# Gate and up products of a decoder layer: features by the row, or tokens by the row with seven block products in place of eight

## The chip, the cores and the metric

The kernel runs on one core of a Trainium2 chip. Its engines are TensorE (PE in the rows; PEld is its load of the stationary operand), VectorE (DVE), ScalarE (ACT), GpSimd (POOL) and the queue that issues the loads (SP). The metric is the device time of one execution in microseconds (us). Before the change the median of three runs is 1202.92 us, from 1201.81 to 1204.26.

## The reference

One decoder layer over 256 tokens of width 2048, in float32. A mixer (a gated linear recurrence beside differential attention) is followed by a norm; then come a SwiGLU network with 5632 hidden features, a second norm, a gate on a per-layer input, and a third norm. The change is in the SwiGLU:

```python
def swiglu(h, w_gate, w_up, w_down):
    g = jnp.einsum('bsd,df->bsf', h, w_gate)
    u = jnp.einsum('bsd,df->bsf', h, w_up)
    return jnp.einsum('bsf,fd->bsd', jax.nn.silu(g) * u, w_down)
...
        h = layer_norm(ALPHA * h + m, ln1_g[i], ln1_b[i])
        f = swiglu(h, w_ffn_gate[i], w_ffn_up[i], w_ffn_down[i])
        h = layer_norm(ALPHA * h + f, ln2_g[i], ln2_b[i])
```

## The kernel before, in words

**Numbers in two parts.** TensorE multiplies rounded operands, so each operand is split into a high and a low part, and a product is three: high by high, high by low, low by high. For a weight the high part `wh` is a copy on ScalarE (L114) and the low part `wl` a subtraction on VectorE (L106), both 1024 columns wide.

**Weight units.** The weights come in units of 128 rows by 2048 columns, 1 MB each, one load per unit on SP (L96) into three buffers. `Stream` splits a unit in halves of 1024 columns. Six pairs of `wh` and `wl` exist, so the high part of a half can be written when TensorE is done with the half six places earlier (`room`, L116).

**Ticks.** The order of the program is the order in which Python emits it; nothing is rescheduled. TensorE's work is cut into quarters of a unit. After each quarter `tick` (L127) emits one stage of every job that is under way (a job is a generator, and a `yield` ends a stage), then the low part of the next half and the high part of the one after it. Each engine works through its own list in order, and waits for others by semaphores.

**Gate and up before.** The 44 tiles of 128 features run in three parts of 16, 16 and 12 (`FPARTS`). `feature_major` (L199) makes the tile's product with features on the rows of the result: for each of 16 row tiles, one instruction with 512 columns (the weight's high part by both parts of `x1`, L196) and one with 256 (the low part by the high part of `x1`, L197). The job `swiglu` (L759) adds the two halves of a bank, applies silu to gate, multiplies by up, and writes both parts of the product into `hT`, which the down projection takes as its stationary operand. The down projection is `token_major` (L226): tokens on the rows, 24 instructions of 512 columns a unit, in two banks.

**Banks.** The pool `pm` has four PSUM banks, taken in turn; `aux` has two, and `sc` is one tile of two banks. The per-layer inputs (`ple_unit`, L731) stand in the `pm` banks and in `sc` just ahead of the SwiGLU, and the script of the first norm (`norm_to`, L651, with `NORM1`) copies them to `ev` in its steps `v` (L695), the last of them in the second tick of the SwiGLU.

## Time and profile before

| | |
|---|---|
| median of three runs | 1202.92 us |
| span of the profiled execution, first to last instruction | 1199.7 us |
| rest of the median around that span | 3.2 us |
| PE busy | 1182.0 us (99%) |
| PEld busy | 1008.2 us (84%) |
| DVE busy | 775.7 us (65%) |
| ACT busy | 607.5 us (51%) |
| POOL busy | 34.3 us (3%) |
| mean DMA rate | 196 GB/s |

The profile lists each instruction with its start and its duration. Instructions of one engine overlap at their ends, so the step from one start to the next is shorter than the duration, and it is the step that adds up. A wait is shown in brackets as the engine's idle time and what ended it. The granted TensorE clock is shown as a share of 2.4 GHz.

### The profile page before, as it was taken

What the parts mean: (1) busy time and instruction counts of PE and PEld (TensorE: products, weight loads), DVE (VectorE), ACT (ScalarE), POOL (GpSimd) and SP (SyncE); (2) the same over time, 40 slices, a digit from 0 to 9 for tenths busy, and PEclk for the clock granted to TensorE, in tenths of its full rate; (3) what the DMA queues carried; (4) which work ended last, traced back from release to release, by engine and by line L of the source; (5) the groups of instructions that cost most, each with busy time, mean ns of one, the idle gap of its engine ahead of it and who ended that gap; (6) DMA issues with size and microseconds to landing.
All of it is one profiled execution on the core that took longest, in us unless ns stands there. A gap on an engine that the chain in (4) does not pass through costs nothing.

```text
span 1199.7 us, 15640 instructions
## 1 busy us (share of the span) xinstructions
PE 1182.0 (99%) x6210; PEld 1008.2 (84%) x6210; DVE 775.7 (65%) x1066; ACT 607.5 (51%) x945; POOL 34.3 (3%) x60
## 2 busy tenths in 40 slices
PE   9999999999999999999999999999999999999995
PEld 7888888888888888888888888888888888887885
DVE  6976988785678555564455555554455555556977
ACT  6767576664456454443335444443344454435640
POOL 0000000001010000000000000000000000002001
PEclk9999999999999999999999999999999999999998
DMA  9765454547638555555555555555555555554741
GB/s 332 263 219 196 174 176 148 181 164 287 235 119 315 183 203 177 200 186 197 189 199 187 176 189 196 176 181 205 186 200 176 190 196 175 182 204 150 281 166 70
DMA packets 38872, 234.83 MB, mean 196 GB/s; under 512 B 4432, under 2 KB 8440, under 8 KB 12048
## 3 DMA queue, kind: packets, MB, share of 16 engines
q1 hardware_dynamic: 35952, 221.51, 52.7%
q0 software_dynamic: 2848, 12.34, 2.7%
q8 instruction: 48, 0.79, 0.2%
q14 instruction: 24, 0.20, 0.0%
HBM read 231.72 MB, written 3.68 MB: 196 GB/s over the span
## 4 chain that ended last, share of the span: by engine, by line
PE 94%; DVE 3%; ACT 1%; POOL 1%; DMA 1%; issue 0%; SPq 0%; DVEq 0%; POOLq 0%; ACTq 0%
PE u L196 13%; PE g L196 13%; PE u L197 7%; PE g L197 7%; PE dps L223 7%; PE dps L224 7%; PE dps L222 6%; PE ops L222 2%; PE ops L223 2%; PE ops L224 2%; PE xr L196 2%; PE k L196 2%; PE yg L196 2%; PE q L196 2%; PE gps L223 2%; PE gps L222 2%
## 5 line engine op out<-in xcount | busy, mean ns | idle before, releaser
L106 DVE TENSOR_TENSOR wl<-w,wh 128x1024 fp32r<-128x1024 f32 x404 | 493.0, 1223 | 277.3 <-ACT wh L114 271.3
L114 ACT CAST wh<-w 128x1024 fp32r<-128x1024 f32 x404 | 423.9, 1052 | 309.3 <-PE dps L224 143.7
L196 PE MATMUL u<-x,wh 128*128 128x512 f32 x688 | 243.4, 396 | 0.0
L196 PE MATMUL g<-x,wh 128*128 128x512 f32 x688 | 243.4, 396 | 0.0
L197 PE MATMUL u<-x,wl 128*128 128x256 f32 x688 | 193.0, 281 | 0.0
L197 PE MATMUL g<-x,wl 128*128 128x256 f32 x688 | 193.0, 281 | 0.0
L196 PEld LDWEIGHTS u<-x,wh 128*128 128x128 f32 x688 | 129.1, 188 | 30.8
L196 PEld LDWEIGHTS g<-x,wh 128*128 128x128 f32 x688 | 129.1, 188 | 30.8
L222 PE MATMUL dps<-wh,hT 128*128 128x512 f32 x352 | 137.1, 389 | 0.0
L224 PE MATMUL dps<-wh,hT 128*128 128x512 f32 x352 | 137.0, 389 | 0.0
L223 PE MATMUL dps<-wl,hT 128*128 128x512 f32 x352 | 137.0, 389 | 0.0
L197 PEld LDWEIGHTS g<-x,wl 128*128 128x128 f32 x688 | 130.0, 189 | 0.1
L197 PEld LDWEIGHTS u<-x,wl 128*128 128x128 f32 x688 | 130.0, 189 | 0.0
L222 PEld LDWEIGHTS dps<-wh,hT 128*128 128x128 f32 x352 | 66.1, 188 | 13.8
L223 PEld LDWEIGHTS dps<-wl,hT 128*128 128x128 f32 x352 | 66.1, 188 | 13.6
L224 PEld LDWEIGHTS dps<-wh,hT 128*128 128x128 f32 x352 | 66.1, 188 | 13.6
L212 ACT COPY g<-g 128x256 f32<-128x256 f32 x43 | 16.0, 372 | 79.4 <-PE g L197 79.4
L212 ACT COPY uu<-u 128x256 f32<-128x256 f32 x43 | 16.0, 373 | 77.0 <-PE u L197 77.0
L222 PE MATMUL ops<-wh,mhl 128*128 128x512 f32 x128 | 50.3, 393 | 0.0
L223 PE MATMUL ops<-wl,mhl 128*128 128x512 f32 x128 | 49.9, 390 | 0.0
L224 PE MATMUL ops<-wh,mhl 128*128 128x512 f32 x128 | 49.9, 390 | 0.0
L196 PE MATMUL xr<-xhl,wh 128*128 128x512 f32 x128 | 46.5, 406 | 1.6 <-ACT wh L71 1.5
(227 smaller groups left out, 1598.6 us busy)
## 6 DMA issues: line engine op xcount, KB each, us to landing
w<-in_w_gate SPq DMA_DIRECT2D x44, 1024.0 KB, 4.9
w<-in_w_up SPq DMA_DIRECT2D x44, 1024.0 KB, 4.8
w<-in_w_down SPq DMA_DIRECT2D x44, 1024.0 KB, 4.9
w<-in_w_a SPq DMA_DIRECT2D x28, 1024.0 KB, 4.9
w<-in_w_out SPq DMA_DIRECT2D x16, 1024.0 KB, 4.9
w<-in_w_pg SPq DMA_DIRECT2D x16, 1024.0 KB, 5.0
w<-in_w_v SPq DMA_DIRECT2D x8, 1024.0 KB, 4.9
lng<-in_ln_g POOLq DMA_DIRECT2D x3, 1024.0 KB, 5.9
```

What stands on the lines that cost most here:

```text
L106: self.nc.vector.tensor_tensor(wl, self.source(self.los), wh.bitcast(F32), ALU.subtract)
L114: self.nc.scalar.copy(wh, src)
L196: nc.tensor.matmul(ps, wh[:, c], xhl[:, k, :], start=(k == 0), stop=False)
L197: nc.tensor.matmul(ps[:, :S], wl[:, c], xhl[:, k, :S], start=False, stop=(k == KT - 1))
L212: nc.scalar.copy(out, ps[:, S:])
L222: nc.tensor.matmul(ps, ah, wh[:, c], start=first, stop=False)
L223: nc.tensor.matmul(ps, ah, wl[:, c], start=False, stop=False)
L224: nc.tensor.matmul(ps, al, wh[:, c], start=False, stop=last)
```

## The change

**Tokens on the rows.** `gate_up` takes four feature tiles at a time (a group, 11 in all). A unit now holds two row tiles of gate and of up for 512 features; it is loaded by two DMAs of 512 KB whose contiguous runs are 1 KB, where there was one with runs of 8 KB. For each row tile, token half and weight, `product` issues three instructions of 512 columns, with `x1` stationary. Four banks `q[token half][gate or up]` hold the sums.

**Seven products.** In the last two of a group's eight units the two row tiles and the two token halves, by gate and up, form a product of 2 by 2 blocks, done with seven block products in place of eight (Strassen's scheme in Winograd's form). Its operands are sums: of `x1`, made once after the first norm (`sums_of_x1`), and of the weights, made on VectorE (`add_up`). Such a unit is split into four parts: gate, one quarter of up, and two of sums. Three of the products go straight into `q`, the others into `p1`, `p6`, `p5`, `p7`.

**The end of a group.** The job `finish` starts in the group's last unit. It adds the banks up, applies silu, multiplies, turns the product by eight transpositions on TensorE (two of four), and splits it into `hT`.

**Room.** `ev` goes to DRAM and comes back after the SwiGLU, since its tiles (tag `T`) hold the sums of weights in between; the sums of `x1` take the place of the norm's `g` and `b` (tag `gb`), and the second norm's are loaded in the third part. Small buffers share one tag of seven (`tmp`).

```diff
+SEVEN = 2
...
-            self.order[2 * n:2 * n + 4] = [(n, 0), (n + 1, 0), (n, 1), (n + 1, 1)]
+        self.sevens = sevens
+        self.order = [(n, j) for n in range(len(srcs)) for j in range(4 if n in sevens else 2)]
...
+            if isinstance(self.srcs[n], tuple):
+                for i, src in enumerate(self.srcs[n]):
+                    dst = w[:, i * 1024:(i + 1) * 1024].rearrange("p (f c) -> p f c", f=4)
+                    self.nc.sync.dma_start(dst, src)
...
+        if n in self.sevens and j:
+            if j == 1:
+                return self.blocks(n)[:, 1, :, 1, :], 512
+            return self.sums[n][:, (j - 2) * 1024:(j - 1) * 1024], 1024
+        return self.w32[n][:, j * 1024:j * 1024 + 1024], 1024
...
+    def add_up(self, n, j):
+        add = lambda out, a, b: self.nc.vector.tensor_tensor(out, a, b, ALU.add)
+        b = self.blocks(n)
+        if j == 0:
+            self.sums[n] = self.sums_pool.tile([P, 2048], F32, tag="T", name="sums", bufs=2)
+        t = self.sums[n].rearrange("p (i f c) -> p i f c", i=4, f=4)
+        if j == 0:
+            w = self.w32[n]
+            diagonal = bass.AP(w.tensor, w.offset, [w.ap[0], [1024 + P, 2], [2 * P, 4], [1, P]])
+            add(t[:, 0:2], diagonal, b[:, 1, :, 0, :].unsqueeze(1).broadcast_to([P, 2, 4, P]))
+        else:
+            t1, t2, t4 = t[:, 0], t[:, 2], t[:, 3]
+            add(t2, t1, b[:, 1, :, 1, :])
+            add(t4, t2, b[:, 0, :, 1, :])
...
+        self.released += j == 1
...
+        self.nc.scalar.copy(self.shaped(wh, src, cols), src)
+        if n in self.sevens and j < 2:
+            self.add_up(n, j)
...
-        srcs += [t[n][f0 + i] for i in range(nf) for n in ("w_gate", "w_up")]
+        for f in range(f0, f0 + nf, 4):
+            sevens.update(range(len(srcs) + PAIRS - SEVEN, len(srcs) + PAIRS))
+            srcs += [tuple(t[w][f:f + 4, :, 2 * P * j:2 * P * (j + 1)].rearrange("f p c -> p f c")
+                           for w in ("w_gate", "w_up")) for j in range(PAIRS)]
...
-                us[h, b] = late.tile([P, 512], F32, tag="u", name="u", bufs=2)
+                us[h, b] = tmp("u")
...
+                elif a == "E":
+                    for h in range(2):
+                        nc.gpsimd.dma_start(evd[h], ev[h])
...
+    def sums_of_x1():
+        xsum.append(late.tile([P, SEVEN, 4, 2, P], F32R, tag="gb", name="xsum"))
+        work = act.tile([P, 2 * SEVEN * 512], F32, tag="A", name="work")
+        x, sums = work[:, :SEVEN * 512], work[:, SEVEN * 512:]
+        ks = slice(KT - 2 * SEVEN, KT)
+        nc.vector.tensor_tensor(x.rearrange("p (k s) -> p k s", s=S), x1[:, ks, :S].bitcast(F32),
+                                x1[:, ks, S:].bitcast(F32), ALU.add)
+        yield
+        a11, a21, a12, a22 = (x.rearrange("p (m i c) -> p m i c", i=4, c=P)[:, :, i, :] for i in range(4))
+        s1, s3, s2, s4 = (sums.rearrange("p (m i c) -> p m i c", i=4, c=P)[:, :, i, :] for i in range(4))
+        nc.vector.tensor_tensor(s1, a22, a21, ALU.subtract)
+        nc.vector.tensor_tensor(s3, a11, a21, ALU.subtract)
+        yield
+        nc.vector.scalar_tensor_tensor(s2, s1, -1.0, a11, ALU.mult, ALU.subtract)
+        nc.vector.tensor_tensor(s4, a12, s2, ALU.add)
+        yield
+        sums = sums.rearrange("p (n c) -> p n c", c=P)
+        hi, lo = (xsum[0].rearrange("p m i a c -> p (m i) a c")[:, :, a, :] for a in range(2))
+        nc.scalar.copy(hi, sums)
+        yield
+        nc.vector.tensor_tensor(lo, sums, hi.bitcast(F32), ALU.subtract)
...
+    def product(ps, a, w, first, last):
+        out = ps.rearrange("p (f c) -> p f c", c=P)
+        nc.tensor.matmul(out, a[0], w[0], start=first, stop=False)
+        nc.tensor.matmul(out, a[0], w[1], start=False, stop=False)
+        nc.tensor.matmul(out, a[1], w[0], start=False, stop=last)
...
+    def gate_up(hT, i0):
+        n0 = st.take(PAIRS)
+        q = [[bank("gu") for _ in range(2)] for _ in range(2)]
+        for m in range(PAIRS - SEVEN):
+            for g in range(2):
+                for h in range(2):
+                    for i in range(2):
+                        k = 2 * m + i
+                        a = [x1[:, k, o + h * P:o + (h + 1) * P] for o in (0, S)]
+                        product(q[h][g], a, operand(n0 + m, g, i), m + i == 0,
+                                g * h * i == 1 and m == PAIRS - SEVEN - 1)
+                    st.free(h)
+                    st.tick()
+        pp = [aux("p1"), aux("p6")]
+        both = pa.tile([P, 2, 512], F32, tag="sc", name="p57")
+        p1, p6, p5, p7 = pp[0], pp[1], both[:, 0, :], both[:, 1, :]
+        for m in range(PAIRS - SEVEN, PAIRS):
+            n, first, last = n0 + m, m == PAIRS - SEVEN, m == PAIRS - 1
+            def x(h, i):
+                return [x1[:, 2 * m + i, o + h * P:o + (h + 1) * P] for o in (0, S)]
+            def sx(i):
+                return [xsum[0][:, m - PAIRS + SEVEN, i, a, :] for a in range(2)]
+            product(q[0][0], x(0, 1), operand(n, 0, 1), False, last)
+            product(p1, x(0, 0), operand(n, 0, 0), first, last)
+            if last:
+                if hT is None:
+                    hT = act.tile([P, KT, 2 * S], F32R, tag="A", name="hT")
+                st.start(finish(hT, i0, q, p1, p6, p5, p7))
+            st.free()
+            st.tick()
+            product(q[0][1], sx(3), operand(n, 1, 0), False, last)
+            st.free()
+            product(p5, sx(0), operand(n, 2, 0), first, last)
+            st.tick()
+            product(p7, sx(1), operand(n, 2, 1), first, last)
+            st.free()
+            product(q[1][0], x(1, 1), operand(n, 3, 1), False, last)
+            st.tick()
+            product(p6, sx(2), operand(n, 3, 0), first, last)
+            st.free()
+            st.tick()
+        return hT
+    def finish(hT, i0, q, p1, p6, p5, p7):
+        add = lambda out, a, b, op=ALU.add: nc.vector.tensor_tensor(out, a, b, op)
+        yield
+        g0 = tmp("g0")
+        nc.scalar.copy(g0, q[0][0])
+        yield
+        u0 = tmp("u0")
+        nc.scalar.copy(u0, q[0][1])
+        add(g0, p1, g0)
+        u1 = tmp("u1")
+        nc.scalar.copy(u1, q[1][1])
+        yield
+        g1, u2, u3 = tmp("g1"), tmp("u2"), tmp("u3")
+        nc.scalar.copy(g1, q[1][0])
+        nc.scalar.copy(u2, p6)
+        nc.scalar.activation(g0, g0, AF.Silu)
+        yield
+        add(u2, p1, u2)
+        add(u3, p7, u2)
+        add(u2, p5, u2)
+        yield
+        add(g1, g1, u3)
+        add(u3, p5, u3)
+        add(u0, u0, u2, ALU.subtract)
+        nc.scalar.activation(g1, g1, AF.Silu)
+        yield
+        add(u1, u1, u3, ALU.subtract)
+        add(g0, g0, u0, ALU.mult)
+        yield
+        add(g1, g1, u1, ALU.mult)
+        for h, g in enumerate((g0, g1)):
+            tp = aux("tp")
+            for i in range(4):
+                nc.tensor.transpose(tp[:, i * P:(i + 1) * P], g[:, i * P:(i + 1) * P], ident)
             yield
+            tp = tp.rearrange("p (a b) -> p a b", b=P)
+            hi, lo = (hT[:, i0:i0 + 4, o + h * P:o + (h + 1) * P] for o in (0, S))
+            nc.scalar.copy(hi, tp)
+            yield
+            nc.vector.tensor_tensor(lo, tp, hi.bitcast(F32), ALU.subtract)
...
-                gps, ups = feature_major(x1, "g"), []
-                st.start(swiglu(gps, ups, hT, i))
-                ups.append(feature_major(x1, "u"))
...
+        for i0 in range(0, nf, 4):
+            hT = gate_up(hT, i0)
         nq = nf // 4
         end = part == len(FPARTS) - 1
+        if end:
+            gb = load_gb(2)
...
+    ev = [late.tile([P, D], F32, tag="T", name="ev", bufs=2) for _ in range(2)]
...
+    ev = [late.tile([P, D], F32, tag="T", name="ev", bufs=2) for _ in range(2)]
+    for h in range(2):
+        nc.gpsimd.dma_start(ev[h], evd[h])
```

On TensorE, where one group ends and the next begins (in words: the last product of a group is `p6`, here `p_3714`; behind it come 24 instructions of the next group and then the first transposition). Before, the list holds the two forms of `feature_major` at this place:

```order
L197 MATMUL u<-x_3149,wl 128x256
L196 MATMUL u<-x_3149,wh 128x512
L197 MATMUL u<-x_3149,wl 128x256
L196 MATMUL g<-x_3149,wh 128x512
L197 MATMUL g<-x_3149,wl 128x256
L196 MATMUL g<-x_3149,wh 128x512
```

After, around the first transposition of the first group's product:

```order
L847 MATMUL gu<-wl,x_3150 128x512
L848 MATMUL gu<-wh,x_3150 128x512
L846 MATMUL gu<-wh,x_3150 128x512
L847 MATMUL gu<-wl,x_3150 128x512
L848 MATMUL gu<-wh,x_3150 128x512
L939 MATMUL tp<-ident,g_3774 128x128 x4
L846 MATMUL gu<-wh,x_3150 128x512
L847 MATMUL gu<-wl,x_3150 128x512
L848 MATMUL gu<-wh,x_3150 128x512
```

The pairs of 512 and 256 columns are gone, all are 512, and TensorE has a row of four transpositions that reads `g0` of the group just ended, 24 instructions into the next.

On VectorE, at the end of a feature tile before (`g` and `uu` are gate and up, `hT` the low part of the product):

```order
L214 TENSOR_TENSOR g<-g 128x256
L106 TENSOR_TENSOR wl<-w_3695,wh 128x1024
L106 TENSOR_TENSOR wl<-w_3744,wh 128x1024
L214 TENSOR_TENSOR uu<-u,uu 128x256
L768 TENSOR_TENSOR g<-g,uu 128x256
L106 TENSOR_TENSOR wl<-w_3744,wh 128x1024
L772 TENSOR_TENSOR hT<-g,hT 128x256
L106 TENSOR_TENSOR wl<-w_3791,wh 128x1024
```

After, from the end of the first group's last product to `g0`'s product with up (`p_3713` is `p1`, `p_3715` is the tile of `p5` and `p7`, `u_3802` and `u_3803` are `u2` and `u3`, `g_3774` is `g0`, `g_3801` is `g1`, `u_3789` and `u_3792` are `u0` and `u1`):

```order
L147 TENSOR_TENSOR wl<-w_3660,wh 128x1024 x2
L907 TENSOR_TENSOR u_3802<-p_3713,u_3802 128x512
L907 TENSOR_TENSOR u_3803<-p_3715,u_3802 128x512
L907 TENSOR_TENSOR u_3802<-p_3715,u_3802 128x512
L147 TENSOR_TENSOR wl<-w_3734,wh 128x1024
L907 TENSOR_TENSOR g_3801<-g_3801,u_3803 128x512
L907 TENSOR_TENSOR u_3803<-p_3715,u_3803 128x512
L907 TENSOR_TENSOR u_3789<-u_3789,u_3802 128x512
L147 TENSOR_TENSOR wl<-w_3734,wh 128x1024
L907 TENSOR_TENSOR u_3792<-u_3792,u_3803 128x512
L907 TENSOR_TENSOR g_3774<-g_3774,u_3789 128x512
L907 TENSOR_TENSOR g_3801<-g_3801,u_3792 128x512
```

Where two or three additions stood between two low parts, seven additions of 512 columns, two products and the low parts of weights now stand in one run, and the row that the first transposition reads (`g_3774`, L907, next to last) is the tenth row, counted from the first that reads `p1` and `u2`.

On ScalarE, at the same place, after (`gu` is a bank of `q`, `p_3714` is `p6`; before, a copy of a bank, a silu or a high part of `hT`, all of 256 columns, stood between two high parts of weights):

```order
L156 CAST wh<-w_3660 128x1024
L913 COPY u_3789<-gu 128x512
L916 COPY u_3792<-gu 128x512
L156 CAST wh<-w_3660 128x1024
L919 COPY g_3801<-gu 128x512
L920 COPY u_3802<-p_3714 128x512
L921 ACT_TABLE_LOAD
L921 ACTIVATE g_3774<-g_3774 128x512
L156 CAST wh<-w_3734 128x1024 x2
L930 ACTIVATE g_3801<-g_3801 128x512
```

The copies out of five banks and two silu now stand between the high parts of the next group's weights.

## Rows read from the trace of the kernel before

**Rows 1.** Page, the chain that ended last, share of the span by engine.
```profile
PE 94%; DVE 3%; ACT 1%; POOL 1%; DMA 1%; issue 0%; SPq 0%; DVEq 0%; POOLq 0%; ACTq 0%
```

**Rows 2.** Windows: stage, length, busy of PE, PEld, DVE, ACT, POOL; clock, DMA, GB/s.
```profile
359.40:536.99 177.59, 177.59 (x1028) 156.59 (x1026) 110.69 (x136) 91.84 (x135) 1.14 (x2) 1.00 0.59 210
536.99:624.07 87.08, 87.08 (x387) 72.07 (x385) 44.18 (x42) 34.41 (x34) 0.00 (x0) 1.00 0.56 194
624.07:804.96 180.89, 180.89 (x1026) 156.96 (x1024) 103.98 (x127) 86.79 (x126) 0.00 (x0) 1.00 0.54 186
804.96:892.06 87.10, 87.10 (x386) 72.10 (x385) 44.17 (x42) 34.42 (x34) 0.00 (x0) 1.00 0.57 195
892.06:1027.73 135.67, 135.67 (x769) 117.72 (x768) 77.94 (x95) 64.92 (x94) 0.00 (x0) 1.00 0.54 186
```

**Rows 3.** Timeline of PE, 354 to 360 us: start, duration, instruction.
```profile
354.86 0.39 PE L224 MATMUL eps<-wh,phl 128*128 128x512 f32 x1
355.15 0.66 PE L681 MATMUL tp<-ident,z 128*128 128x128 f32 x4
355.56 0.48 PE L222 MATMUL eps<-wh,phl 128*128 128x512 f32 x1
355.88 0.40 PE L223 MATMUL eps<-wl,phl 128*128 128x512 f32 x1
...
359.40 0.48 PE L196 MATMUL gu<-x,wh 128*128 128x512 f32 x1
```

**Rows 4.** Timeline of ACT, 359 to 363 us.
```profile
359.83 0.61 ACT L695 COPY ev<-eps 128x512 f32<-128x512 f32 x1
360.31 0.62 ACT L684 CAST x<-tp 128x512 fp32r<-128x512 f32 x1
360.79 1.09 ACT L114 CAST wh<-w 128x1024 fp32r<-128x1024 f32 x1
361.73 1.12 ACT L695 COPY ev<-eps 128x512 f32<-128x512 f32 x2
```

**Rows 5.** Timeline of PE and ACT, 558 to 559 us, down projection.
```profile
558.56 0.39 PE L224 MATMUL dps<-wh,hT 128*128 128x512 f32 x1
...
558.99 1.05 ACT L114 CAST wh<-w 128x1024 fp32r<-128x1024 f32 x1 [1.67 <-PE dps L224]
```

**Rows 6.** Timeline of DVE, 1109 to 1113 us.
```profile
1109.28 0.69 DVE L693 TENSOR_TENSOR x<-y,x 128x512 fp32r<-128x512 f32 x1
1109.89 0.69 DVE L697 TENSOR_TENSOR z<-z,lng 128x512 f32<-128x512 f32 x1
1110.61 0.69 DVE L698 TENSOR_TENSOR z<-z,lnb 128x512 f32<-128x512 f32 x1
1111.21 1.22 DVE L106 TENSOR_TENSOR wl<-w,wh 128x1024 fp32r<-128x1024 f32 x1
1112.35 0.68 DVE L693 TENSOR_TENSOR x<-y,x 128x512 fp32r<-128x512 f32 x1
```

**Rows 7.** Lines by form: busy, mean ns of one, idle before and its releaser.
```profile
L642 DVE TENSOR_TENSOR z<-z,dps 128x512 f32<-128x512 f32 x16 | 10.5, 679 | 3.1 <-PE dps L224 3.1
L764 ACT ACTIVATE g<-g 128x256 f32<-128x256 f32 x44 | 18.5, 420 | 0.4 <-DVE g L214 0.4
L106 DVE TENSOR_TENSOR wl<-w,wh 128x1024 fp32r<-128x1024 f32 x404 | 493.0, 1223 | 277.3 <-ACT wh L114 271.3 <-PE u L196 3.1
```

**Rows 8.** Page's DMA issues and DMA of 9 to 17 us: KB each, us to landing.
```profile
w<-in_w_gate SPq DMA_DIRECT2D x44, 1024.0 KB, 4.9
...
DMA packets 2420, 2.94 MB, mean 367 GB/s; under 512 B 146, under 2 KB 1826, under 8 KB 2420
...
w<-in_w_a SPq DMA_DIRECT2D x3, 384.0 KB, 7.2
```

**Rows 9.** Windows, with the columns of rows 2: a wait in the second norm.
```profile
1090.00:1094.00 4.00, 2.62 (x14) 1.74 (x13) 2.83 (x4) 1.21 (x3) 3.33 (x4) 1.00 0.00 0
```

More of the change, by code (lines that the diff above doesn't have):

```diff
@@ L108, in prepare_lo @@
+    def prepare_lo(self):
+        n, j = self.order[self.los]
+        wh, wl = self.parts[n, j]
+        src, cols = self.source(self.los)
+        wh, wl = (self.shaped(t, src, cols) for t in (wh, wl))
+        self.nc.vector.tensor_tensor(wl, src, wh.bitcast(F32), ALU.subtract)
+        self.released += j == 1
         self.los += 1
@@ L649, in residuals, with norm_to @@
             yield
-    def norm_to(script, xhl, pss, scale, stats, gb, cols):
+    def norm_to(script, xhl, pss, scale, stats, gb, cols, then=None):
         mvs, us, tps = {}, {}, {}
@@ L694, in step @@
             elif what == "v":
-                nc.scalar.copy(ev[:, h, c], inputs[b][h])
+                nc.scalar.copy(ev[h][:, c], inputs[b][h])
             elif what == "r":
@@ L711, in norm_to @@
         st.held = False
+        if then is not None:
+            yield from then()
     gb = load_gb(1)
@@ L774, in tile_hybrid_layer @@
-    for part, (f0, nf) in enumerate(FPARTS):
-        hT = act.tile([P, KT, 2 * S], F32R, tag="A", name="hT")
-        for i in range(nf):
-            if part == 0 and i == 0:
-                gps, ups = feature_major(x1, "gu", 2)
-                st.start(swiglu(gps, [ups], hT, i))
-                gb = load_gb(2)
-            else:
-                gps, ups = feature_major(x1, "g"), []
-                st.start(swiglu(gps, ups, hT, i))
-                ups.append(feature_major(x1, "u"))
+    def product(ps, a, w, first, last):
[3 more added lines that the diff above has]
+        nc.tensor.matmul(out, a[1], w[0], start=False, stop=last)
@@ new lines, in operand @@
+    def operand(n, j, i):
+        parts = st.half(n, j)
+        if n in st.sevens and j:
+            return [w[:, i * 512:(i + 1) * 512].rearrange("p (f c) -> p f c", c=P) for w in parts]
+        return [w.rearrange("p (f k c) -> p f k c", f=4, k=2)[:, :, i, :] for w in parts]
+    def gate_up(hT, i0):
[40 more added lines that the diff above has]
+        return hT
@@ L810, in gated @@
         n = cols.stop - cols.start
[L811 removed]
+        g = tmp("pg")[:, :n]
         nc.vector.tensor_tensor(g, ps[:, :n], pb[:, cols], ALU.add)
```

73 lines of the change are left out of this document (33 added, 40 removed).

## Prediction

> **What bounds the kernel now.** I read the chain of waits first: 94% of the span lies on TensorE and 1% on loads [rows 1]. The windows by stage come next: in all three gate/up stages and in the down stages between them TensorE is busy for the whole stage at the full clock, VectorE for 57 to 62% in gate and up (110.69 of 177.59 us, 103.98 of 180.89, 77.94 of 135.67) and ScalarE for about half [rows 2]. So before the change time goes by TensorE's instructions alone, and a change pays there if it takes instructions off TensorE and adds no wait in front of one. The later rows price both.
>
> **The matmuls.** A down stage is 16 units of 24 instructions of 512 columns, 384 in 87.08 us [rows 2]: 0.2268 us each. The three gate/up stages last 177.59 + 180.89 + 135.67 = 494.15 us for 88 units [rows 2]. After the change these units are instructions of the same 512 columns with x1 stationary, 24 a unit, so I price them like those of the down stage. 66 units of 24 and 22 units of 21 make 2046, and 2046 x 0.2268 = 464.0 us. The gain is 30.1 us. Half of it comes from the form (2112 x 0.2268 = 479.0, 15.2 us less than 494.15), half from the 66 instructions that Strassen's scheme drops (15.0 us). The weights are now read in runs of 128 columns and the result is written as four such runs; no row shows that form, and I take the price of the plain one.
>
> **The transpositions.** Each group adds eight, in two rows of four. Around such a row of four in the first norm, the matmul before starts at 354.86 and the second one behind at 355.88 [rows 3]: 1.02 us where two steps would be 0.45, so 0.57 us a row. 22 rows at 0.55 make 12.1 us.
>
> **The wait in front of the first transposition.** This is the term that decides. The transposition of g0 is emitted four ticks into the next group, 24 x 0.2268 = 5.44 us after TensorE leaves the group's last product p6. By then VectorE must have run the ten rows of its list from the addition of p1 and u2 to the product of g0 and u0, which the list after the change shows, two low parts of weights among them. I count from TensorE's end of p6.
> ScalarE starts 0.43 us after the start of the matmul that it waits for (558.99 against 558.56) [rows 5], so 0.20 us after the step ends. Its copy of p6 to u2 starts at 0.20 at the earliest and takes 0.60: done at 0.8 [rows 4]. What stands before it on ScalarE doesn't hold it much longer: from the release of a half at -4.56 (21 instructions earlier, and 0.20 for the release) it runs a high part, a copy, a high part and two copies; with steps of 0.94 for a high part and 0.48 for a copy (360.79 to 361.73, 360.31 to 360.79) [rows 4] the last high part starts at -1.24, the copy of q10 at -0.30, that of p6 at 0.2. VectorE's low part for that last high part runs from -0.16, and the next row may start 1.14 later [rows 6], at 1.0.
> VectorE's steps: 0.61 from one 512-column row to an independent one, 0.72 to one that needs its result, 1.14 for a low part [rows 6]. The addition to u2 takes 0.72 (the next needs it), the two others 0.61 each, a low part 1.14, three additions 1.83, a low part 1.14, an addition 0.61, and the last row, the product, its full 0.69: 7.35 us. An addition that reads PSUM lasts 0.68 as well [rows 7], so I make no difference between them. VectorE is done at 1.0 + 7.35 = 8.35, TensorE arrives at 5.44: it waits 2.9 us. It happens at each of the 11 groups, also where the down projection follows, since a tick is six instructions there too: 31.9 us.
> From below: with every row independent, starting at 0.8, the sum is 0.8 + 7 x 0.61 + 2 x 1.14 + 0.69 = 8.0, a wait of 2.6. From above: each addition with a handover (0.74), each low part at its full 1.22, and ScalarE late by one high part (0.94) give 1.9 + 5.2 + 2.4 + 0.7 = 10.2, a wait of 4.8. I take 2.9, by the steps as the rows show them, and keep 28 and 53 us as ends. Behind the first transposition stand the second (12 instructions later, its product is one row further on VectorE, ready at about 9) and the next units, whose halves are ready by then; they add nothing. The silu of g1 (0.42 us for 256 columns [rows 7], an estimate of 0.8 at most for 512) ends before the product that needs it.
>
> **The start.** The four banks of the first group are those in which the per-layer inputs stood, and the third, q[1][0], is needed after six instructions, not after two units. TensorE began at 359.40 [rows 3], so it wants the bank at 360.9; the last two copies to ev run from 361.73 for 1.12 us [rows 4]. A wait of 2.0 us, once.
>
> **What I cost at nothing.** Per group VectorE has 12 low parts of plain units, and for each of the two special ones three of 1024 and one of 512 columns, one sum of 1024 and two of 512; with ten rows and two low parts at the end that is 20 rows at 1.14 and 18 at 0.61, 34 us of some 46. So it keeps up over a group, and the backlog of the wait is gone before the next special units; uncovered, a late half costs its 1.14 us on TensorE. The sums of x1 have some 30 us before their first use. The way of ev to DRAM and back on POOL's queue stands behind the second norm's first scale and ahead of its second, with room of several microseconds; the ends of both norms are otherwise the same. The loads keep their bytes, 1 MB per unit, but half of the three buffers' lead goes in the special units: the load of the third unit of the next group is issued some 7 us before its first high part, and a load lands in 4.9 us [rows 8].
> The loads are now two of 512 KB in runs of 1 KB. At the start, where loads of 384 KB in runs of up to 1 KB fill the queue, the DMA engines moved 367 GB/s [rows 8], and gate and up need 186 to 210 [rows 2], so I add nothing. The Trainium skill (DMA: Bandwidth & Descriptors, section "Bandwidth") advises DMAs of 1 MiB and more and shows far lower rates for small ones, 138 GB/s at 64 KB; at that rate, an estimate by the page, a unit would take 7.6 us to land where TensorE needs 5.44, and loads would become the bound. The trace speaks against it, since the queue overlaps neighbouring loads.
>
> **The sum.** -30.1 + 12.1 + 31.9 + 2.0 = +15.9 us on the profiled span of 1199.7 us. The median of the runs is 3.2 us over that span, so 1202.9 + 15.9 = 1218.8 us. With the ends of the wait (28 and 53), 11 to 13 for the transpositions and 1 to 3 for the start, the likeliest case runs from +10 to +39: 1213 to 1242.
>
> **The rivals.**
> A, faster. TensorE doesn't wait at the transposition. The point from which it decides is 16.0 / 11 = 1.45 us a group: VectorE must finish the product within 6.9 us of p6. VectorE's idle time in gate and up (some 40%) [rows 2] speaks for it, of which nearly all is a wait for ScalarE's high parts (271.3 of 277.3 us before the low parts) [rows 7], so low parts may be done earlier than I count; against it stands that the ten rows can't start before p6 is copied, whatever went before. Without any wait: -30.1 + 12.1 + 2.0 = -16.0, 1187 us.
> B, no change. The wait is half as long, as if the two low parts were out of the way: 8.35 - 2.28 = 6.1, a wait of 0.6, or of 1.5 with ScalarE late by one high part. With 11 such waits 1194 to 1204 us, about 1202.
> C, slower still. The special units starve too: eight halves (9.1 us of low parts) fall due in their 9.5 us, with ScalarE's five copies between, and a load that comes late holds ScalarE's list and all behind it. One high and low part per group, 2.2 us, makes +24: 1243 us.
> D, the clock. Each wait lets TensorE fall to the 1.2 GHz level. In the second norm it stood idle for 1.4 of 4 us and the granted clock stayed 1.00 [rows 9]; if instead six instructions a group ran at half the clock, that adds 1.36 x 11 = 15 us: 1234. The Trainium skill (TensorE: Matmul & The Clock Gate, section "HAM oscillation") has a kernel whose regular idle gaps brought the clock down each time; no wait as long as 2.9 us with work on both sides is in this trace.
>
> **How the numbers follow.** Forecast 67%, A 14%, B 7%, C 9%, D 3%. The time is 1218.8 us. B, the nearer part of A, D and the forecast's own range up to 1240 are taken into the range, 1200 to 1240, which leaves out some 12% below and 7% above. What this kernel's measurement can tell from no change is about 0.2%, 2.4 us. Faster: A and three of B's seven, 17%. Same: the rest of B and 2% of the forecast's lower edge, 6%. Slower: 77%.
>
> **What would show it.** Matmuls of gate and up at steps of 0.227 us, 2046 of them; transpositions with TensorE idle 2.5 to 3.5 us before the first of each group, released by VectorE's product (L907), and none before the second; no wait on a DMA; PEclk at 1.00 throughout; 2 us of idle time at the second bank block of the first group, released by the copy to ev. It would be wrong if the first transposition found g0 ready, if the matmuls with weights in runs of 128 columns took longer than 0.227, or if TensorE waited on halves of weights in the special units.

## The result and the profile after

The changed kernel takes 1235.76 us (median of four runs, 1234.59 to 1236.05), the kernel before 1202.44 us on the same chip (four runs): a ratio of 1.0265, 95% interval 1.025 to 1.0279. It is slower by 33.3 us, where the forecast was 1218.8 us, slower by 15.9. The time lies in the range, the sign is right, and the loss is a little over twice the forecast's. The span grew from 1199.7 to 1233.8 us, by 34.1.

The page of the kernel after: busy time of TensorE, its granted clock in 40 slices, and the chain of waits, the counterpart of [rows 1].
```profile
PE 1179.6 (96%) x5528; PEld 981.0 (80%) x5528; DVE 879.1 (71%) x1138; ACT 633.0 (51%) x913; POOL 36.0 (3%) x64
...
PEclk9999999999999999999999999999999999999998
...
PE 83%; DVE 10%; ACT 4%; issue 2%; POOL 1%; DMA 0%; SPq 0%; DVEq 0%; ACTq 0%; POOLq 0%
```
TensorE's part of the chain fell from 94 to 83%, and VectorE now holds 10%. The clock by slices looks untouched, since a slice is 31 us long: a fall of a few microseconds does not show there. The waits of TensorE say where VectorE comes in (total us, times, longest):
```profile
PE tp L939 <- DVE g L907: 36.2, 11, 4.1
```
There is one wait for each of the 11 groups, in front of the first transposition, and it ends with VectorE's product (L907), as the prediction named it. TensorE waits for nothing else in the SwiGLU, neither a half of a weight nor a load. The loads of 512 KB land fast (page: KB each, us to landing):
```profile
w<-in_w_gate SPq DMA_DIRECT2D x88, 512.0 KB, 3.6
w<-in_w_up SPq DMA_DIRECT2D x88, 512.0 KB, 4.7
```
The windows by stage, with the columns of [rows 2]: gate and up of the first part, and its down projection.
```profile
359.15:545.97 186.82, 176.32 (x772) 145.19 (x771) 143.19 (x157) 99.12 (x120) 1.15 (x2) 0.97 0.59 193
545.97:638.65 92.68, 89.46 (x393) 73.84 (x392) 52.16 (x52) 37.44 (x39) 0.00 (x0) 0.98 0.56 196
```
Against [rows 2] the gate and up stage lost 9.2 us and the down stage 5.6. The down stage loses because the last group of its part is transposed there. The granted clock is 0.97 and 0.98, where it was 1.00. TensorE's timeline behind the second group shows both losses (start, duration, instruction, and in brackets the idle time before it and what ended it):
```profile
455.49 0.39 PE L848 MATMUL gu<-wh,x 128*128 128x512 f32 x1
459.08 1.08 PE L939 MATMUL tp<-ident,g 128*128 128x128 f32 x4 [3.21 <-DVE g L907]
459.82 0.77 PE L846 MATMUL gu<-wh,x 128*128 128x512 f32 x1
460.39 0.63 PE L847 MATMUL gu<-wl,x 128*128 128x512 f32 x1
460.82 0.63 PE L848 MATMUL gu<-wh,x 128*128 128x512 f32 x1
461.25 0.63 PE L846 MATMUL gu<-wh,x 128*128 128x512 f32 x1
461.67 0.53 PE L847 MATMUL gu<-wl,x 128*128 128x512 f32 x1
462.04 0.39 PE L848 MATMUL gu<-wh,x 128*128 128x512 f32 x1
...
463.43 0.39 PE L848 MATMUL gu<-wh,x 128*128 128x512 f32 x1
463.66 0.60 PE L939 MATMUL tp<-ident,g 128*128 128x128 f32 x4
...
464.33 0.39 PE L847 MATMUL gu<-wl,x 128*128 128x512 f32 x1
```
The transposition should start at 455.49 + 0.23 = 455.72 and starts at 459.08, 3.36 us late. Then four instructions follow each other by 0.43 us (460.39, 460.82, 461.25, 461.67) where the step is 0.23 at the full clock: TensorE runs at half speed for some 3 us. From the first transposition to the second lie 4.58 us; twelve matmuls at 0.2268 and a row of transpositions at 0.45 are 3.17, so 1.4 us are lost a second time. At the other groups the same stretch takes 4.5 to 4.8 us. The granted clock in the 6 us behind the first transposition of the second and the last group:
```profile
459.08:465.08 6.00, 6.00 (x25) 5.04 (x26) 3.68 (x5) 2.32 (x4) 0.00 (x0) 0.76 0.65 209
...
1065.30:1071.30 6.00, 6.00 (x24) 4.87 (x25) 3.41 (x4) 2.10 (x4) 0.00 (x0) 0.72 0.87 292
```
The other nine read 0.72 to 0.77; over all eleven the mean is 0.73. Six microseconds at 0.73 of the clock are 1.6 us lost, some 17.6 us for 11 groups. PE counts as busy all this time (6.00 of 6.00 us): here busy time does not show the slow clock, the steps and the clock column do.

VectorE's timeline ahead of that transposition, for the length of the wait:
```profile
450.20 1.23 DVE L147 TENSOR_TENSOR wl<-w,wh 128x1024 fp32r<-128x1024 f32 x1 [0.39 <-ACT wh L156]
451.34 2.20 DVE L907 TENSOR_TENSOR u<-p,u 128x512 f32<-128x512 f32 x3
453.46 1.21 DVE L147 TENSOR_TENSOR wl<-w,wh 128x1024 fp32r<-128x1024 f32 x1
454.59 0.68 DVE L907 TENSOR_TENSOR g<-g,u 128x512 f32<-128x512 f32 x1
455.31 0.69 DVE L907 TENSOR_TENSOR u<-p,u 128x512 f32<-128x512 f32 x1
455.92 0.68 DVE L907 TENSOR_TENSOR u<-u,u 128x512 f32<-128x512 f32 x1
456.52 1.22 DVE L147 TENSOR_TENSOR wl<-w,wh 128x1024 fp32r<-128x1024 f32 x1
457.65 0.68 DVE L907 TENSOR_TENSOR u<-u,u 128x512 f32<-128x512 f32 x1
458.26 1.28 DVE L907 TENSOR_TENSOR g<-g,u 128x512 f32<-128x512 f32 x2
```
VectorE has almost no idle time here; TensorE waits for a list that simply is as long as this. The step of p6 ends on TensorE at 455.72 - 5.44 = 450.28. The list starts 1.06 us later (forecast 1.0), and from 451.34 to the end of the first of the two products, 458.26 + 0.69 = 458.95, it takes 7.61 us (forecast 7.35).

### The profile page after: what moved, and what is told of

Read it like the earlier page. It is cut to its first block, busy times and chain, and to the rows that moved or that the text cites. A ratio compares the mean times of both kernels' runs of the same rounds, so it can differ in the third digit from the quotient of the medians.

```text
span 1233.8 us, 14610 instructions
## 1 busy us (share of the span) xinstructions
PE 1179.6 (96%) x5528; PEld 981.0 (80%) x5528; DVE 879.1 (71%) x1138; ACT 633.0 (51%) x913; POOL 36.0 (3%) x64
## 4 chain that ended last, share of the span: by engine, by line
PE 83%; DVE 10%; ACT 4%; issue 2%; POOL 1%; DMA 0%; SPq 0%; DVEq 0%; ACTq 0%; POOLq 0%
PE gu L846 10%; PE gu L847 10%; PE gu L848 10%; PE dps L271 6%; PE dps L269 6%; PE dps L270 6%; DVE wl L147 4%; PE ops L269 2%; PE ops L270 2%; PE ops L271 2%; DVE u L907 2%; PE xr L243 2%; PE yg L243 2%; PE k L243 2%; PE q L243 2%; PE gps L270 2%
## 5 line engine op out<-in xcount | busy, mean ns | idle before, releaser
L147 DVE TENSOR_TENSOR wl<-w,wh 128x1024 fp32r<-128x1024 f32 (+1 forms) x404 | 479.6, 1192 | 215.4 <-ACT wh L156 215.0
L156 ACT CAST wh<-w 128x1024 fp32r<-128x1024 f32 (+1 forms) x404 | 413.6, 1031 | 342.8 <-PE dps L271 129.3
L846 PE MATMUL gu<-wh,x 128*128 128x512 f32 x572 | 229.1, 400 | 0.0
L847 PE MATMUL gu<-wl,x 128*128 128x512 f32 x572 | 227.1, 397 | 0.0
L848 PE MATMUL gu<-wh,x 128*128 128x512 f32 x572 | 226.5, 396 | 0.0
L848 PEld LDWEIGHTS gu<-wh,x 128*128 128x128 f32 x572 | 110.2, 193 | 23.8
L847 PEld LDWEIGHTS gu<-wl,x 128*128 128x128 f32 x572 | 110.2, 193 | 22.6
L846 PEld LDWEIGHTS gu<-wh,x 128*128 128x128 f32 x572 | 110.0, 192 | 22.5
L147 DVE TENSOR_TENSOR wl<-sums,wh 128x1024 fp32r<-128x1024 f32 x44 | 52.9, 1224 | 50.6 <-ACT wh L156 50.6
L156 ACT CAST wh<-sums 128x1024 fp32r<-128x1024 f32 x44 | 45.2, 1051 | 49.9 <-PE gu L848 41.8
L939 PE MATMUL tp<-ident,g 128*128 128x128 f32 x88 | 15.9, 310 | 36.2 <-DVE g L907 36.2
L943 ACT CAST hT<-tp 128x512 fp32r<-128x512 f32 x22 | 12.9, 587 | 66.4 <-PE tp L939 66.4
```

What stands on the lines that cost most here:

```text
L147: self.nc.vector.tensor_tensor(wl, src, wh.bitcast(F32), ALU.subtract)
L156: self.nc.scalar.copy(self.shaped(wh, src, cols), src)
L846: nc.tensor.matmul(out, a[0], w[0], start=first, stop=False)
L847: nc.tensor.matmul(out, a[0], w[1], start=False, stop=False)
L848: nc.tensor.matmul(out, a[1], w[0], start=False, stop=last)
L939: nc.tensor.transpose(tp[:, i * P:(i + 1) * P], g[:, i * P:(i + 1) * P], ident)
```

## The experiments

The theory is that the 36.2 us of waits come from the length of VectorE's list behind p6, and that each wait also costs 1.4 to 1.6 us of slow clock behind it. The rivals are that the new form of the matmuls or the loads carry part of the loss, and that the slow clock comes from the change's matmuls and not from the waits. All edits are to the kernel after unless another is named; the times of before in those sessions lay between 1201.9 and 1204.6 us, and each ratio is to the runs of before on the same chip.

**The wait taken away.** At ten of the eleven groups the first transposition comes three ticks later, 18 instructions or 4.1 us.
```diff
+        if i0 + f0 < 40:
+            yield 3
         for h, g in enumerate((g0, g1)):
```


> The changed kernel with the transpositions of a group three ticks (18 instructions, 4.1 us) later on TensorE, at 10 of the 11 groups; the last group's stay where they are. Theory (the wait in front of the first transposition is the cost, 3.3 us a group, and the fall of the clock that follows it 1.4): both go at 10 groups, 10 x 4.7 = 47 us less than the changed kernel, about 1189 us; idle time before the transpositions under 5 us in all, granted clock back over 0.99. Rival (VectorE or the loads can't keep up with a group, so the time comes back elsewhere): under half of it, over 1212 us, with new waits of TensorE for parts of weights. Rival (only the wait goes, the slow stretch has another cause): 1202 us.


Measured: 1185.79 us, ratio 0.9849 (0.9826 to 0.9873); the mean clock of the profiled execution is 0.997. One edit turns a loss of 2.7% into a gain of 1.5%. The last group, left as it was, still waits, and its rows hold a surprise:
```profile
1015.40 0.63 PE L941 MATMUL tp<-ident,g 128*128 128x128 f32 x4 [3.22 <-DVE g L907]
1015.79 0.48 PE L269 MATMUL dps<-wh,hT 128*128 128x512 f32 x1
1016.11 0.39 PE L270 MATMUL dps<-wl,hT 128*128 128x512 f32 x1
```
The same wait of 3.2 us, and yet no slow matmul behind it: 0.32 us to the next, 0.23 from there on, and a granted clock of 1.00 in the eight microseconds that follow. So the length of a wait alone does not say whether the clock falls.

**The wait filled.** In place of idling, TensorE multiplies zeros into the bank that the transposition then overwrites. The transposition comes as late as before; only the idling is gone (at the first group, with its longer wait, 0.96 us of idling is left).
```diff
             tp = aux("tp")
+            for i in range(14 if h == 0 else 0):
+                nc.tensor.matmul(tp, zero[:, :P], zero, start=True, stop=True)
```


> The changed kernel with 14 matmuls of zeros (512 columns, about 0.21 us each, 3.0 us) ahead of each group's first transposition, into the bank that the transposition then overwrites; they fill the wait with work that nothing uses. Theory (idle TensorE loses its clock, 1.4 us a group): the clock stays up, the wait itself (3.3 us) is only covered, 11 x 1.4 = 15 us less than the changed kernel, about 1220 us, clock over 0.99. Rival (the slow stretch belongs to the transpositions or to the restart, not to the clock): no gain, 1233 to 1240 us.


Measured: 1219.42 us, ratio 1.0129 (1.0105 to 1.0153), mean clock 0.996 (after: 0.982). The second group again:
```profile
455.54 0.39 PE L848 MATMUL gu<-wh,x 128*128 128x512 f32 x1
455.77 3.19 PE L939 MATMUL tp<-zero 128*128 128x512 bf16 x13
459.05 0.66 PE L941 MATMUL tp<-ident,g 128*128 128x128 f32 x4
459.46 0.48 PE L846 MATMUL gu<-wh,x 128*128 128x512 f32 x1
459.77 0.39 PE L847 MATMUL gu<-wl,x 128*128 128x512 f32 x1
```
The transposition starts at 459.05 (after: 459.08), as late as in the kernel after, but the two matmuls behind it follow at 0.41 and 0.31 us (after: 0.74 and 0.57). This isolates the clock: idling at the wait costs 1235.76 - 1219.42 = 16.3 us on top of the wait, 1.5 us a group. The traces alone say the same: 32 instructions from the start of the first transposition take 7.7 to 8.0 us in the kernel after and 6.4 to 6.5 us here, 16.2 us over the 11 groups.

**The list made shorter.** The two low parts are put off until the recombination is done.
```diff
+        st.held = True
         yield
         add(u2, p1, u2)
...
         add(g1, g1, u1, ALU.mult)
+        st.held = False
```


> The changed kernel with no weight prepared in the three ticks in which VectorE does a group's additions, so that the two low parts (2 x 1.14 us) stand behind the product that the first transposition reads. Theory (the wait is the length of VectorE's list from the copy of p6 on): it shrinks from 3.3 to about 1.0 us a group, and a wait so short leaves the clock up: 11 x (2.3 + 1.4) = 41 us less, about 1195 us. Rival (VectorE is short of time over the whole group): the low parts are late for the next units instead, TensorE waits for them, and less than 15 us is gained.


Measured: 1193.41 us, ratio 0.9914 (0.9892 to 0.9937). The wait's total falls by 26.5 us, where two low parts at 1.14 in 11 groups are 25.1:
```profile
PE tp L941 <- DVE g L907: 9.7, 11, 1.1
```
Together with the late transposition this settles the wait: it is the list's length against the distance in the program, and either end of it can be moved. Waits of 1.1 us and less left the mean clock at 0.995.

**The form alone.** Tokens on the rows, but eight block products everywhere, with the short end of a group that goes with them.
```diff
-SEVEN = 2
+SEVEN = 0
...
+                        st.start(finish(hT, i0, q), 2)
...
-                st.start(finish(hT, i0, q, p1, p6, p5, p7))
```


> Gate and up with tokens on the rows, but with all eight block products (no sums of x1 or of weights) and a short end of a group: silu from the bank, one product a token half, transpositions three ticks into the next group. Theory: 2112 instructions at 0.2268 are 479.0 us, 15 less than before the change, the transpositions cost 22 x 0.45 = 10 us, VectorE's list is two rows long so nothing waits: 5 us less than before the change, about 1197 us. Rival (the form itself is the cost: runs of 128 columns, 1 KB runs in the loads, transpositions): 1205 us or more.


Measured: 1197.39 us, ratio 0.9949 (0.9929 to 0.9969), no wait at the transpositions. So the new form is not where time is lost; with its transpositions it gives 7 us by itself (before: 1204.37 us on the same chip).

**All waits out.** The late transposition at all groups; at the last one, where nothing but the down projection follows, the first two column blocks of the down projection take turns, so that the row tiles of `hT` that come late are needed later.
```diff
+        yield 3
         for h, g in enumerate((g0, g1)):
...
+LAST01 = [(0, 0), (0, 1), (1, 0), (1, 1), (0, 2), (1, 2)]
```


> e1 with the last group's transpositions three ticks later as well; so that the down projection may wait for them, its last part does the first two row quarters of both first column blocks before the third of either (the order of those six units alone changes). Theory: the one wait that e1 left (3.2 us, the clock stayed up behind it) goes: about 1182 us. Rival: the last units' order costs something of its own at the second norm: 1185 us or more.


Measured: 1181.75 us, ratio 0.9807 (0.9786 to 0.9829), span 1178.8, no wait for VectorE at a transposition. Against the eight products everywhere that is 15.6 us, where the prediction had 15.0 for the 66 instructions that the scheme drops.

**One tick later only.** It separates the wait from the clock at another length.
```diff
+        if i0 + f0 < 40:
+            yield 1
```


> e1 with one tick (1.36 us) in place of three, at 10 groups: the wait in front of the transposition should be 3.3 - 1.4 = 1.9 us. Theory of the wait alone: 10 x 1.4 = 14 us less than the changed kernel, 1222 us, if the clock still falls behind each wait; 10 x (1.4 + 1.4) = 28 less, 1208 us, if a wait of 1.9 us leaves it up. Rival (the time goes elsewhere): no relation to the ticks, over 1225 us.


Measured: 1207.82 us (ten runs), ratio 1.0033 (1.0017 to 1.0049). The second group and its clock:
```profile
456.30 0.39 PE L848 MATMUL gu<-wh,x 128*128 128x512 f32 x1
458.53 0.63 PE L941 MATMUL tp<-ident,g 128*128 128x128 f32 x4 [1.85 <-DVE g L907]
458.92 0.48 PE L846 MATMUL gu<-wh,x 128*128 128x512 f32 x1
```
```profile
454.00:464.00 10.00, 8.15 (x40) 6.49 (x39) 9.65 (x13) 4.90 (x7) 0.00 (x0) 1.00 0.61 198
```
A wait of 1.9 us, and the clock stays at 1.00. Moving the transposition by 1.36 us at ten groups takes 13.6 us off the waits (36.2 to 22.6), but 27.9 us off the time: the other 14 are the clock, which in this trace stays up at all eleven groups. That includes the first, with a wait of 2.7 us, and the last, left as it was:
```profile
1039.07 0.63 PE L941 MATMUL tp<-ident,g 128*128 128x128 f32 x4 [3.22 <-DVE g L907]
```
Behind this wait, too, the clock is 1.00 for six microseconds, so the first experiment's row is no single case. Only one execution was traced; the ten lie between 1205.94 us at a mean clock of 0.996 and 1211.33 us at 0.991, so the clock did not stay up as well in all of them.

**More pairs with seven products.** On the kernel without waits, three and then four of the eight pairs.
```diff
-SEVEN = 2
+SEVEN = 3
```


> The kernel of e5 with three of eight row-tile pairs as seven block products in place of two (SEVEN = 3). Theory (TensorE is the bound again once the transpositions wait for nothing): 33 x 3 x 0.2268 = 7.5 us less than e5, about 1175 us. VectorE gets per group 7 rows for 2 and stands at about 39 of 42 us. Rival (VectorE's burst in the special units holds TensorE): waits of TensorE for low parts or transpositions appear and the gain is under 3 us or turns into a loss.

> The kernel of e5 with four of eight (SEVEN = 4). TensorE's own work falls by 15 us against e5, but VectorE's list of a group is about 43 us by its steps (8 x 1.14 for plain low parts, 4 x 6.4 for the special units, 8 for the end of the group), and TensorE's 41.7. Theory: VectorE becomes the bound, TensorE waits in every group for low parts of weights, and the time is no better than with three, 1172 to 1190 us. Rival (the steps overlap better): 1167 us.


Measured: with three 1181.60 us (ratio 0.9808, 0.9787 to 0.9828), no better than with two; with four 1196.44 us (0.9931, 0.991 to 0.9952), 15 us worse. With three the rival held. With four the time lies above all that was expected, 1190 us at most. With three pairs the wait at the transposition is back, 5.4 us, though VectorE's list behind p6 is the same ten rows of 7.60 us at most groups; no sum of weights stands in it. What changed is its start, 2.30 us behind p6 where it was 1.06, since VectorE comes to it through a row of low parts and has had no idle time for eight microseconds. At the second group p6 ends at 445.27, and the list starts at
```profile
447.57 2.21 DVE L911 TENSOR_TENSOR u<-p,u 128x512 f32<-128x512 f32 x3
```
With four pairs it starts 3.5 us behind p6, and the wait is larger:
```profile
PE tp L944 <- DVE g L911: 17.4, 11, 1.8
```
What this left open is whether VectorE is full or only wrongly ordered. Three runs took this up, all on the kernels with three or four pairs.
```diff
-        yield 3
+        yield late_by
...
+            hT = gate_up(hT, i0, 4 if i0 + 4 < nf or f0 == FPARTS[-1][0] else 3)
```


> Three of the eight row-tile pairs take seven block products, and the first transposition of a group comes four ticks late (three at the ends of parts 0 and 1) where it was three. Theory (the 5.4 us of waits for VectorE's last sums in the run with three pairs are a place in the program only): these waits go and the time falls from 1181.6 to about 1177 us. Rival (the waits show that VectorE's list is now as long as its cover, so that it ends late elsewhere, at the second half of the group): 1181 us or more.

> Three of the eight pairs take seven products, the first transposition three ticks late, and VectorE makes no weight sums while it closes a group's recombination. Theory (the list before the last sum is what is waited for): its 7.6 us fall to about 4.5, the 5.4 us of waits go, 1175 to 1178 us. Rival (the weight sums that are put off come too late for the next products): PE waits for wl instead, 1181 us or more.

> Four of the eight pairs take seven products, the first transposition three ticks late, no weight sums on VectorE while it closes a group. Theory (the 17.4 us of waits with four pairs come from the weight sums in VectorE's last list, as with three pairs, where this took 7.5 us off for 5.4 us of waits): 1196.4 falls by 17 to 25 us, to 1172 to 1180 us, with waits for g under 4 us. Rival (with four pairs VectorE is late throughout, so that what is put off comes back as products that wait for wl): 1188 us or more.


The edit shown is that of the first; the others put `st.held` around the additions, as above, which takes the two low parts out of the list (7.60 to 5.33 us at most groups). So what their expectations call weight sums in VectorE's last list are low parts in the trace. Measured: three pairs and four ticks 1175.38 us (0.9769, 0.9743 to 0.9796); three pairs and the short list 1174.08 us (0.9762, 0.9738 to 0.9785), 1.6 and 0.9 us below what the theory gave; four pairs and the short list 1180.36 us (0.9796, 0.9778 to 0.9815), 0.4 us above the theory's upper end. With three pairs it was the order of the work. With four the wait at the transposition is gone from the list of waits, but products wait for low parts:
```profile
PE p L851 <- DVE wl L148: 2.2, 13, 0.2
PE gu L851 <- DVE wl L148: 2.0, 6, 0.4
```
and the first gate and up stage shows VectorE busy for 182.45 of 183.80 us (the third busy time, behind those of PE and PEld):
```profile
359.20:543.00 183.80, 180.57 (x791) 144.22 (x791) 182.45 (x207) 116.73 (x144) 1.15 (x2) 1.00 0.62 206
```
In this stage some 40 steps between matmuls are over 0.25 us, 8.2 us too long together; with three pairs there are 8 of them, all at transpositions, and 0.7 us, with VectorE busy for 166.70 of 178.80 us. So in the first stage the fourth pair finds VectorE full. The two other gate and up stages have 20 and 15 such steps, 3.4 and 2.4 us too long, and last as long as with three pairs (169.1 against 168.9 us, 126.6 against 126.4): the fourth pair's saving is lost in them as well.

**Weight sums on GpSimd.** Four pairs; `add_up` runs on the engine that is nearly idle.
```diff
-        add = lambda out, a, b: self.nc.vector.tensor_tensor(out, a, b, ALU.add)
+        add = lambda out, a, b: self.nc.gpsimd.tensor_tensor(out, a, b, ALU.add)
```


> Four of the eight pairs take seven products, the first transposition three ticks late, and GpSimd makes the weight sums in place of VectorE. Theory (with four pairs VectorE's list is the bound: 17.4 us of waits for g and about 7 us of late products in the first part): these go and the time falls from 1196.4 to 1170 to 1180 us. Rival (GpSimd's adds are slower than VectorE's or hold VectorE up, so that weight sums come late): 1190 us or more, with PE waiting for wl.


Measured: 1251.97 us, ratio 1.0411 (1.0383 to 1.0438), slower by 55 us than with the sums on VectorE. The rival held, on both counts: GpSimd is slower, and VectorE is held up. TensorE waits 33.0 us at the transpositions and 24.7 us for low parts, and the mean clock is 0.979. Lines by form of this kernel (mean ns of one is the second number):
```profile
L129 POOL TENSOR_TENSOR sums<-sums,w 128x512 f32<-128x512 f32 x88 | 166.9, 1896 | 6.9
L148 DVE TENSOR_TENSOR wl<-sums,wh 128x1024 fp32r<-128x1024 f32 x88 | 147.0, 1707 | 4.7 <-ACT wh L157 4.4
...
L129 POOL TENSOR_TENSOR sums<-w 128x1024 f32<-128x1024 f32 x44 | 132.1, 3003 | 400.2 <-DMA w<-in_w_up 326.3 <-DVE wl L148 55.9 <-DVE u L911 17.2
...
L911 DVE TENSOR_TENSOR g<-g,u 128x512 f32<-128x512 f32 x33 | 39.9, 1235 | 0.0
```
and of the kernel with the sums on VectorE:
```profile
L148 DVE TENSOR_TENSOR wl<-sums,wh 128x1024 fp32r<-128x1024 f32 x88 | 103.8, 1218 | 16.9 <-ACT wh L157 16.9
...
L129 DVE TENSOR_TENSOR sums<-sums,w 128x512 f32<-128x512 f32 x88 | 60.5, 687 | 1.5
L129 DVE TENSOR_TENSOR sums<-w 128x1024 f32<-128x1024 f32 x44 | 53.6, 1217 | 0.0
...
L911 DVE TENSOR_TENSOR g<-g,u 128x512 f32<-128x512 f32 x33 | 21.6, 683 | 0.0
```
GpSimd takes 1896 and 3003 ns for what VectorE does in 687 and 1217. And VectorE's own operations are longer meanwhile: the operations that write g 1235 ns instead of 683, the low parts of sums 1707 instead of 1218. VectorE gave away 114 us of work and was busier for it, 1027.9 us instead of 963.5. That the additions beside it are the cause shows within this trace: the low parts of `w` of 1024 columns that had no addition of GpSimd beside them took 1219 ns (298 of them), those that lay wholly beside one 2480 ns (34); the operations that write g took 684 (17) and 1907 ns (14). The Trainium skill (GPSIMD Engine Reference, section "Performance versus the Vector engine") gives an add of two float32 operands of 2048 columns as 1.96 times as long on GpSimd as on VectorE. Here the means are 2.5 and 2.8 times as long at 1024 and 512 columns, and the shortest addition of 1024 columns, 2385 ns, 1.96 times.

## Why the prediction was right in sign and short by 17 us

**The matmuls, -30.1: right.** In the kernel with zeros in the wait, 17 steps lie between 451.69 and 455.54 us, 0.2265 each, and the price taken from the down projection was 0.2268; the form of 128-column runs costs nothing more here. The kernel without waits tests the term with the transpositions: -30.1 + 9.9 = -20.2 on the span, measured 1178.8 - 1199.7 = -20.9.

**The transpositions, +12.1: a little high.** From 463.43 to 464.33 are 0.90 us for what would be two steps, so a row costs 0.45 and 22 rows 9.9 us. The 0.57 of [rows 3] was measured in the first norm, and did not carry over.

**The wait, +31.9: right in place, cause and nearly in size.** 36.2 us on the profile's own count. The start of the list was 1.06 for 1.0; the list was 7.61 for 7.35, because two more of its additions than I counted take the longer step (454.59 to 455.31 is 0.72, and three additions from 451.34 take 2.12 where I had 1.94): each is followed by one that overwrites what it reads. And 0.13 us from VectorE's end to TensorE's start were left out. The wait is 3.2 us at ten groups and 4.1 at the first. There ScalarE loads the table of silu for 1.28 us, ahead of the high part for which a low part in VectorE's list then waits (0.51 us idle); the list takes 8.20 us, and starts 1.34 us behind p6. Counting a list behind the product that feeds it, row by row with steps and not with durations, was good to an eighth.

**The start, +2.0: wrong, 0.** The third bank's first matmul does not wait:
```profile
360.40 0.39 PE L848 MATMUL gu<-wh,x 128*128 128x512 f32 x1
360.63 0.40 PE L846 MATMUL gu<-wh,x 128*128 128x512 f32 x1
```
although the last copies to `ev` run on ScalarE only from 361.48:
```profile
361.48 1.11 ACT L744 COPY ev<-eps 128x512 f32<-128x512 f32 x2
```
I had given `q[1][0]` the bank that is copied last. The step that failed is this assignment. The likely reason, which no row shows since the trace does not number the banks, is that the pool hands banks out in the order in which they come free in the program, so that this bank goes to a sum that is needed later.

**Weights and loads, costed at nothing: right.** TensorE has no wait for a half of a weight and none for a load, in the special units either. The Trainium skill (DMA: Bandwidth & Descriptors, section "Bandwidth") advises 1 MiB and more to a DMA. That did not bear on this: a unit in two loads of 512 KB lands in 3.6 and 4.7 us, in one it took 4.9 [rows 8].

**The clock: the step that failed.** D, "each wait lets TensorE fall to the 1.2 GHz level", was priced well: 1.36 us a group and 15 us, against 1.5 and 16.3 measured, and its 1234 us is 1.8 us from the time. But the forecast put the clock at nothing ("PEclk at 1.00 throughout"), and D was given 3%, as a rival to the forecast. It is no rival: it comes on top of the wait, and given the wait it was the question. The only evidence against it was a row in which TensorE stood idle for 1.4 of 4 us at a clock of 1.00 [rows 9], and the waits of 1.9 us in the trace of the one tick later leave the clock up too. That row could say nothing of 2.9 us, and the same paragraph said that no such wait is in the trace. With no row on either side it deserved near an even chance. The Trainium skill (TensorE: Matmul & The Clock Gate, section "HAM oscillation") tells of a kernel whose regular idle gaps brought the clock down each time. The trace after agrees with that at all eleven groups. In two other traces the wait of 3.2 us at the last group, with no fall at the groups ahead of it, left the clock at 1.00, and so did the regular waits of 1.9 us.

Without the clock the forecast holds: the kernel with the wait filled took 1219.42 us, the forecast was 1218.8. That it holds to a microsecond is luck, since errors cancel: -2.2 at the transpositions, -2.0 at the start, +4.3 at the waits. And the time lies in the range, 1200 to 1240, because of the slow clock; the range reached so high for a longer wait and for D.

The account of the span: -30.1 for the matmuls, +9.9 for the transpositions, +36.2 for the waits, +16.3 for the clock make +32.3 of 34.1. Most of the rest is that the first transposition starts 3.36 us late at the second group, where the profile counts 3.21 as idle: 0.15 at eleven groups is 1.6.

**The rivals.** A, no wait, is what the kernel with all waits out is: 1181.75 us where A had 1187, of which the transpositions (2.2 us) and the start (2.0) explain 4.2. B and C found nothing in the trace of the kernel after. B's condition, the two low parts out of the way, is that of the kernel with the shorter list: waits of 0.9 us on average and 1193.41 us, just under B's 1194 to 1204.

## What to carry to other kernels

Where one engine is busy without a gap, a saving on it is worth its steps, and everything is decided by the first new wait in its list. Count the list of the engine that feeds it from the last result that it needs, then move the consumer later or move unrelated work out of that list; here the one was worth 54 us at all groups and the other 42, against a saving of 30. Ask also when the feeding engine gets to that list: with three pairs the list had not grown, it began later.

Price a new wait on TensorE as the wait and, as a case of its own with a fair chance where the trace has no wait as long, a stretch at half speed behind it (here some 3 us, at a cost of 1.5). A wait that can't be moved can be filled with multiplications whose result nobody reads. The best version found, three of eight pairs with the low parts out of the last list, takes 1174.08 us, 2.4% less than before. TensorE has no gap in its gate and up stages, and VectorE is 93% busy in the first of them; a fourth pair brought nothing more (1180.36 us).

## What the runs showed of the hardware that was not expected

- The clock behind a wait: waits of 3.2 to 4.1 us at eleven groups were each followed by 0.72 to 0.77 of the full clock over 6 us, with steps of 0.43 us. In the first four groups the clock was down before the wait ended (0.91 to 0.95 over the four microseconds ahead of the transposition), in the others it fell behind it, up to four matmuls later. With the sums on GpSimd the clock also fell at all six waits of 4.2 to 4.3 us.
- In other traces, waits at a transposition left the clock at 1.00: those of 1.1 us and less, of 1.9 and of 2.7 us, and two of 3.2 us, both at the last group (first experiment, and one tick later). Early in the program, at its first projections, a wait of 1.46 us in the kernel with the wait filled was followed by a clock of 0.57 over 4 us, and one of 2.44 us in the kernel after by 1.00. So the length of a wait alone did not decide; what did stays open.
- On VectorE, an addition that overwrites what the one before it reads starts 0.72 us behind it, at all 11 groups, like one that needs the result (0.72 in [rows 6]; 0.79 for the first addition of the list), against 0.61 for an independent one.
- VectorE's work on two operands in SBUF took on average 1.4 to 1.8 times as long in the kernel in which GpSimd adds beside it (1218 to 1707 ns, 683 to 1235 ns), and twice and more where it lay wholly beside an addition, so that moving 114 us of work off VectorE made it busier. The subtractions that read one operand from PSUM (L950, `hT`) kept their 678 ns, also the four that lay wholly beside one.
